# Loads and gathers pinned to the program's order, weight writes in 32 parts

## The chip, the cores and the metric

One core of one Trainium2 chip runs one program. The metric is the device time of an execution in microseconds (us). Of the kernel before there are three runs; the profile is a fourth execution with the hardware profiler on. The program is written with a scheduler that places each engine's instructions itself, out of an estimate of when their inputs are ready; the order in which the program traces them is only a priority, unless an edge is added.

## What is computed

A transformer block over 512 tokens of width 2048 in float32: adaptive norm, a mixer (forgetting attention and a gated linear recurrence), and a feed-forward part with 16384 experts, of which each token uses 16 in each of 8 heads. The change lies in the last:

```python
def _peer(h, w_q, k1, k2, u, vt):
    q = (h @ w_q).reshape(B, S, PEER_HEADS, 2, PEER_HALF)
    s1, s2 = (einsum of q's halves with k1 and with k2)
    ...                     # top 16 of each, top 16 of the 256 sums
    e = expert numbers      # 8 heads x 16 for each token
    w = softmax of the sums
    def expert_block(hx, ex, wx):
        ug = jnp.take(u, ex, axis=0)
        act = jax.nn.gelu(jnp.einsum('thkd,td->thk', ug, hx)) * wx
        vg = jnp.take(vt, ex, axis=0)
        return jnp.einsum('thk,thkd->td', act, vg)
```

## The kernel before

Matrix products run as three passes over float32 values that are split into a high part (cast by ScalarE, L93) and a low part (subtracted by VectorE, L94). `stream` (L96) loads 512 KB into `raw` (four slots) and splits it into `shi` and `slo` (three slots each).

For three of the four groups of 128 tokens the kernel doesn't gather rows of u. It multiplies all of u with the tokens: 128 blocks of 128 experts, `ublock` (L682). A block is two streamed halves of `peer_u`, 24 matmuls each (L689), into a PSUM bank of the two named pj; then gelu on ScalarE (L693), and two writes of the result `ge` to tables in memory through SyncE's queue, to tab2 (L695) and to tab1 (L697). `ublocks(upto)` runs blocks until that number; its calls are spread over the program, so that blocks are traced between other work. This is the block stage, about 1085 to 2385 us.

Beside the blocks run:

- The side work for the fourth group of tokens: 256 gathers of 128 rows (1 MB each) by GpSimd (L743, L766), each used by one VectorE instruction (L755 or L757). `pump`, called after each half of a block, releases 0.9 of them on average, and one scatter.
- `halves_of` (L896): the routing weights of 64 tokens over all experts, `ws`, made by one-hot matmuls (L912) and copied by ScalarE (L913), written to the tables by four writes of 1 MB in rows of 256 bytes (L917) and reduced by VectorE (L918). It is called for three groups, two halves each, with one buffer for `ws`.
- `make_list` (L832): for each row of 128 experts of a block, the numbers of the blocks in use, sorted by 16 rounds of `V.max` and `V.match_replace` (`rounds`, L818), and 16 or 20 scatters of list entries by GpSimd (`one`, L882); `done` (L886) reads the list back through SyncE.
- A top-k for the third group's scores, read back from memory in eight loads (L931).

After the last block the rows of v are gathered chunk by chunk and multiplied (L988). The scheduler decides what stands where in SyncE's list: peer_u loads, writes of ge, writes of ws and the small loads all go through it.

Of the kernel before, what the change touches and what calls it, by code (L numbers as in the profile page):

```python
# [27 lines left out]
LISTS = ((48, 16, 4), (66, 20, 5))  # L28
NONE = 24
B0 = 3  # L30
BH = 18
BL = 20
GRATE = 0.9
GLAG = 2
NAR = 5
# [23 lines left out]
def program(ctx: ExitStack, tc: tile.TileContext, a):  # L59
    nc = tc.nc  # L60
    V, A, PE, G = nc.vector, nc.scalar, nc.tensor, nc.gpsimd
# [31 lines left out]
        A.copy(hi, src)  # L93
        V.tensor_tensor(out=lo, in0=src, in1=hi, op=OP.subtract)  # L94

    def stream(src, n=1024):  # L96
        r = raw.tile([128, 1024], F32, name="raw")
        nc.sync.dma_start(r[:, :n], src)
        hi = hl.tile([128, 1024], F32R, name="shi")
        lo = hl.tile([128, 1024], F32R, name="slo")  # L100
        hilo(hi[:, :n], lo[:, :n], r[:, :n])
        return hi, lo
# [32 lines left out]
    for half in range(2):  # L135
        r = raw.tile([128, 1024], F32, name="raw")[:1]
# [34 lines left out]
    for q in range(4):  # L171
        p = pbank()
# [7 lines left out]
    with tc.tile_pool(name="pro", bufs=1, reuse_waits="tile") as pro:  # L180
# [7 lines left out]
        for t in range(NT):  # L188
# [7 lines left out]
            r = rstd(pro, ss, 1, 1.0 / D)  # L196
            dg = pro.tile([128, 128], F32, name="dg", bufs=2)
            V.tensor_scalar(dg, ident, r, None, op0=OP.mult)
            for k4 in range(4):
                p = pbank()  # L200
# [62 lines left out]
    p = pbank()  # L263
# [9 lines left out]
    p = bank()  # L273
# [245 lines left out]
    for q in range(4):  # L519
# [8 lines left out]
        for k2 in range(KC // 2):  # L528
            w = stream(a["w_out"][q, k2])
# [8 lines left out]
        for t in range(NT):  # L538
# [10 lines left out]
            if q == 3:  # L549
                s4 = const.tile([128, 1], F32, name="s4", bufs=4)  # L550
                V.tensor_reduce(s4, ssq[:, t], axis=AX.X, op=OP.add)
                w = const.tile([128, 128], F32, name="dg", bufs=4)
# [6 lines left out]
    with tc.tile_pool(name="wk2", bufs=12, reuse_waits="tile") as wk2:  # L559
        for q in range(4):  # L560
            pr = bank()
            for k4 in range(4):
                k = q * 4 + k4
                p = bank()
# [80 lines left out]
    for h in range(H):  # L645
# [6 lines left out]
        for half in range(2):  # L652
            p = pbank()
            for hv in range(2):
                wh, wl = stream(a["w_q"][h * 2 + half, hv])
                for k8 in range(8):
                    k = hv * 8 + k8
# [6 lines left out]
            p = bank()  # L664
            c0 = half * 128
# [16 lines left out]
    def ublock(b):  # L682
        p = pbank()
        for half in range(2):
            uh, ul = stream(a["peer_u"][b, half])
            for k8 in range(8):
                k = half * 8 + k8
                for i, (l, r) in enumerate(three(uh, ul, dh[k], dl[k])):
                    PE.matmul(p[:, :NDT], l[:, k8 * 128:k8 * 128 + 128], r, start=(k == 0 and i == 0),  # L689
                              stop=(k == KC - 1 and i == 2))  # L690
            pump()
        ge = gq.tile([128, NDT], F32, name="ge")
        A.activation(ge, p[:, :NDT], AF.Gelu_apprx_tanh)  # L693
        rows = slice(128 + b * 128, 256 + b * 128)
        nc.sync.dma_start(tab2[rows].rearrange("p (t x) -> p t x", t=2)[:, :, 0:128],  # L695
                          ge[:, 128:384].rearrange("p (t x) -> p t x", t=2))
        nc.sync.dma_start(tab1[rows, 0:128], ge[:, 0:128])  # L697
# [5 lines left out]
    blk = [0]  # L703
    todo = []
# [5 lines left out]
    def ublocks(upto):  # L710
        while blk[0] < upto:
            ublock(blk[0])
            blk[0] += 1
# [9 lines left out]
    ei = late.tile([128, H * 16], I32, name="ei")  # L723
# [16 lines left out]
    tabs = (tab2, tab1)  # L740

    def gather(out, src, idx):
        G.indirect_dma_start(out=out, out_offset=None, in_=src,  # L743
                             in_offset=bass.IndirectOffsetOnAxis(ap=idx, axis=0))

    NSIDE = 2 * H * 16 + GLAG

    def side_work():
        held = []
        n = H * 16  # L750

        def use():
            v, j, r = held.pop(0)
            if v:
                V.scalar_tensor_tensor(out=y0, in0=r, scalar=dots[:, j:j + 1], in1=y0, op0=OP.mult, op1=OP.add)  # L755
                return
            V.scalar_tensor_tensor(out=r, in0=r, scalar=1.0, in1=hrow, op0=OP.mult, op1=OP.mult,  # L757
                                   accum_out=dots[:, j:j + 1])
            if j == n - 1:
                A.activation(dots, dots, AF.Gelu_apprx_tanh)  # L760
                V.tensor_tensor(out=dots, in0=dots, in1=ew, op=OP.mult)

        for v in range(2):
            for j in range(n):
                r = gb.tile([128, D], F32, name="gr")
                gather(r, a["v_rows" if v else "u_rows"], ei[:, j:j + 1])  # L766
                held.append((v, j, r))
                if len(held) > GLAG:
                    use()
                yield  # L770
        while held:
            use()
            yield
# [16 lines left out]
    def scatter_some(n):  # L790
        for _ in range(n):
            if scatters:
                scatters.pop(0)()

    todo.append(lambda: side.send(GRATE))
    todo.append(lambda: scatter_some(1))
    for t in (1, 2):
# [20 lines left out]
    def rounds(L, vals, n):  # L818
        for k in range(n):
            sl = slice(k * 8, k * 8 + 8)  # L820
            V.max(L[:, sl], vals[k % 2])
            V.match_replace(vals[1 - k % 2], L[:, sl], vals[k % 2], 0.0)
        return vals[n % 2]

    def rows_of(L, n, nm):
# [6 lines left out]
    def make_list(lt, Fs, n):  # L832
        c0, r, _ = LISTS[n]
        own = []
        cnt = lt.tile([128, 2], F32, name="lcnt")
        vals = [lt.tile([128, 128], F32, name=f"lv{i}") for i in range(2)]
        L = lt.tile([128, 128], F32, name="lf")
# [5 lines left out]
        else:  # L843
# [4 lines left out]
            for i, f in enumerate(fs):  # L848
                rest = rounds(L, [f, vals[0]], NONE // 8)
                ig, iv = rows_of(L, NONE, f"own{i}")  # L850
# [7 lines left out]
        ig, iv = rows_of(L, 128, n)  # L858
# [3 lines left out]
        p = bank()  # L862
# [13 lines left out]
        idx = lp1.tile([128, 32], I32, name=f"lidx{n}")[:, :r]  # L876
# [3 lines left out]
        sv = lp1.tile([128, r], I32, name=f"sv{n}")  # L880

        def one(i):  # L882
            G.indirect_dma_start(out=views[i], out_offset=bass.IndirectOffsetOnAxis(ap=idx[:, i:i + 1], axis=0),
                                 in_=ig[:, c0 + i:c0 + i + 1], in_offset=None, bounds_check=128 * r - 1, oob_is_err=False)

        def done():  # L886
            nc.sync.dma_start(sg, lists[n].rearrange("(p c) o -> p (c o)", p=128))
# [5 lines left out]
    TH = 64  # L893
    sets = {}

    def halves_of(dz, t, o, tab, c0, lo, step):  # L896
        Fs = []
        for hf in range(2):
            h0 = hf * TH
            ws = dz.tile([128, NB, TH], F32, name="ws")  # L900
            for t4 in range(TH // 4):
                ublocks(lo + hf * step + t4 * (step - 3) // (TH // 4))
                p = bank()
                o1 = dz.tile([128, 4, 128], F32, name="o1", bufs=2)
                t0 = h0 + t4 * 4
                V.tensor_tensor(out=o1, in0=iota[:, None, :].to_broadcast([128, 4, 128]),
                                in1=o[:, 0, t0:t0 + 4, None].to_broadcast([128, 4, 128]), op=OP.is_equal)
                for j in range(4):
                    tt = t0 + j
                    o2 = dz.tile([128, 128], F32, name="o2", bufs=6)  # L910
                    V.tensor_scalar(o2, iota, o[:, 1, tt:tt + 1], o[:, 2, tt:tt + 1], op0=OP.is_equal, op1=OP.mult)
                    PE.matmul(p[:, j * 128:j * 128 + 128], o2, o1[:, j], start=True, stop=True)  # L912
                A.copy(ws[:, :, t4 * 4:t4 * 4 + 4].rearrange("p i t -> p t i"), p.rearrange("p (t i) -> p t i", t=4))  # L913
            F = dz.tile([128, NB], F32, name="F", bufs=4)
            for i in range(4):
                sl = slice(i * 32, i * 32 + 32)
                nc.sync.dma_start(tab[128 + i * 4096:4224 + i * 4096, c0 + h0:c0 + h0 + TH].rearrange("(i p) t -> p i t", p=128), ws[:, sl])  # L917
                V.tensor_reduce(F[:, sl], ws[:, sl], axis=AX.X, op=OP.max)  # L918
            Fs.append(F)
        V.tensor_tensor(out=Fs[0], in0=Fs[0], in1=Fs[1], op=OP.max)  # L920
        return Fs[0]
# [191 lines left out]
    r = inv(1)  # L1113
# [75 lines left out]
```

## Time and profile before

| | |
|---|---|
| median of three runs | 3143.48 us (3142.44 to 3146.86) |
| the profiled execution, its span | 3144.75 us, 3142.9 us |
| TensorE busy | 2872.5 us (91%) |
| VectorE busy | 2487.0 us (79%) |
| ScalarE, GpSimd busy | 1220.9 us (39%), 944.1 us (30%) |
| loads of peer_u | 256 of 512 KB |
| writes of ge | 128 of 128 KB, 128 of 64 KB |
| writes of ws | 24 of 1 MB |
| gathers of the side work, scatters | 256, 36 |

In the rows PE is TensorE, PEld its weight loads, DVE VectorE, ACT ScalarE, POOL GpSimd, SP SyncE; a q behind the name is that engine's sequencer, where DMAs are issued and waits are held. L12 is line 12 of the kernel. A row names output<-input by the program's names. "[1.37 <-DMA ...]" is the engine's idle time ahead of the instruction and what ended it. PEclk is the granted clock of TensorE, 1.00 for 2.4 GHz and 0.50 for 1.2 GHz.

### The profile page before, as it was taken

How to read it: one execution, taken by the hardware profiler on the slowest of the kernel's cores; microseconds unless marked ns; L12 is line 12 of the kernel's file. 1: busy time of each engine (PE TensorE's matmuls, PEld its weight loads, DVE VectorE, ACT ScalarE, POOL GpSimd, SP SyncE). 2: the span in 40 equal slices, each digit the busy share in tenths (PEclk: the TensorE clock that was granted, in tenths of full speed). 3: DMA queues.
4: the chain of work that ended last, by engine and by line, in shares of the span. 5: the costliest groups of instructions: out<-in, count | busy, mean ns of one | idle time of the engine just before them, and what ended most of it. 6: DMA issues, size and time to landing. Idle time of an engine off the chain costs nothing.

```text
span 3142.9 us, 39160 instructions
## 1 busy us (share of the span) xinstructions
PE 2872.5 (91%) x14093; PEld 2501.5 (80%) x14093; DVE 2487.0 (79%) x4100; ACT 1220.9 (39%) x1653; POOL 944.1 (30%) x673
## 2 busy tenths in 40 slices
PE   7899999989999999988878999889998899988887
PEld 5677777778788899988868999879996688766665
DVE  6877777763368899999989998968888866677787
ACT  5322223662232333433322343413223455556665
POOL 0000000000020033222242322264447645567774
PEclk9999899999999999999988999989999999999998
DMA  9867777333322389999989999989999977779896
GB/s 343 291 222 235 239 236 238 106 107 128 114 90 94 117 297 379 340 306 295 294 270 357 351 347 352 314 319 404 404 403 386 386 278 272 260 270 344 320 327 228
DMA packets 329503, 869.31 MB, mean 277 GB/s; under 512 B 125682, under 2 KB 181362, under 8 KB 274388
## 3 DMA queue, kind: packets, MB, share of 16 engines
q0 software_dynamic: 72512, 477.03, 40.4%
q1 hardware_dynamic: 256352, 389.52, 36.8%
q8 instruction: 112, 1.84, 0.2%
q14 instruction: 91, 0.75, 0.1%
q10 hardware_dynamic: 436, 0.18, 0.0%
HBM read 805.38 MB, written 61.25 MB: 276 GB/s over the span
## 4 chain that ended last, share of the span: by engine, by line
PE 53%; DVE 17%; DMA 15%; issue 8%; ACT 3%; POOL 2%; SPq 1%; DVEq 0%; POOLq 0%; ACTq 0%
PE pj L689 25%; DMA araw<-w_ada 8%; PE ps L988 7%; PE pj L659 6%; DVE slo L94 5%; PE ps L525 4%; DVE gr L757 3%; PE pj L301 2%; PE ps L219 2%; DMA raw<-tab,ig 2%; DVE araw L147 2%; PE ps L912 2%; PE pj L988 1%; PE pj L525 1%; DMA tab<-ws 1%
## 5 line engine op out<-in xcount | busy, mean ns | idle before, releaser
L689 PE MATMUL pj<-dh,slo 128*128 128x384 f32 x2048 | 698.3, 343 | 59.4 <-DVE slo L94 57.9
L689 PE MATMUL pj<-dh,shi 128*128 128x384 f32 x2048 | 699.1, 341 | 29.0 <-ACT shi L93 26.4
L689 PE MATMUL pj<-dl,shi 128*128 128x384 f32 x2048 | 694.8, 339 | 1.3 <-issue 1.3
L93 ACT CAST shi<-raw 128x1024 fp32r<-128x1024 f32 (+1 forms) x402 | 418.3, 1048 | 634.1 <-PE pj L689 219.0
L94 DVE TENSOR_TENSOR slo<-raw,shi 128x1024 fp32r<-128x1024 f32 (+1 forms) x402 | 485.1, 1214 | 214.3 <-ACT shi L93 200.1
L689 PEld LDWEIGHTS pj<-dh,slo 128*128 128x128 f32 x2048 | 392.1, 192 | 70.6 <-DVE slo L94 68.7
L94 DVE TENSOR_TENSOR slo<-gr,shi 128x1024 fp32r<-128x1024 f32 x342 | 407.2, 1220 | 39.6 <-ACT shi L93 38.1
L689 PEld LDWEIGHTS pj<-dh,shi 128*128 128x128 f32 x2048 | 393.0, 192 | 30.9 <-ACT shi L93 27.9
L93 ACT CAST shi<-gr 128x1024 fp32r<-128x1024 f32 x342 | 345.0, 1046 | 157.0 <-PE ps L988 99.2
L743 POOL DMA_INDIRECT gr<-u_rows,ei x128 | 196.0, 1531 | 690.5 <-DVE gr L757 319.6
L689 PEld LDWEIGHTS pj<-dl,shi 128*128 128x128 f32 x2048 | 392.3, 192 | 2.1 <-issue 2.0
L988 PE MATMUL ps<-shi,gh 128*128 128x512 f32 x740 | 277.7, 418 | 64.3 <-ACT gh L93 36.7
L147 DVE SCALAR_TENSOR_TENSOR araw<-araw,sil 128x1024 f32<-128x1024 f32 x192 | 233.7, 1222 | 104.8 <-DMA araw<-w_ada 101.5
L755 DVE SCALAR_TENSOR_TENSOR y<-gr,dots,y 128x2048 f32<-128x2048 f32 x128 | 300.3, 2346 | 13.9 <-DMA gr<-v_rows,ei 12.6
L988 PE MATMUL ps<-slo,gh 128*128 128x512 f32 x740 | 298.0, 411 | 14.6 <-DVE slo L94 13.8
L743 POOL DMA_INDIRECT gr<-v_rows,ei x128 | 211.7, 1654 | 311.4 <-DVE y L755 204.6
L757 DVE SCALAR_TENSOR_TENSOR gr<-gr,hrow 128x2048 f32<-128x2048 f32 x128 | 291.5, 2279 | 11.3 <-DMA gr<-u_rows,ei 8.8
L988 PE MATMUL ps<-shi,gl 128*128 128x512 f32 x740 | 273.8, 401 | 2.1 <-DVE gl L94 2.1
L678 POOL CAST dh<-hh 128x384 fp32r<-128x384 f32 x16 | 10.3, 645 | 857.8 <-DVE hh L572 857.8
L693 ACT ACTIVATE ge<-pj 128x384 f32<-128x384 f32 x128 | 63.0, 492 | 459.0 <-PE pj L689 371.1
L988 PEld LDWEIGHTS ps<-shi,gh 128*128 128x128 f32 x740 | 145.5, 198 | 112.2 <-ACT gh L93 45.7
L301 PE MATMUL pj<-hh,shi 128*128 128x512 f32 x528 | 215.6, 408 | 3.9 <-ACT w L477 3.5
(353 smaller groups left out, 4966.7 us busy)
## 6 DMA issues: line engine op xcount, KB each, us to landing
raw<-peer_u SPq DMA_DIRECT2D x256, 512.0 KB
araw<-w_ada SPq DMA_DIRECT2D x192, 512.0 KB
raw<-w_in SPq DMA_DIRECT2D x66, 512.0 KB
tab<-ws SPq DMA_DIRECT2D x24, 1024.0 KB
raw<-w_out SPq DMA_DIRECT2D x32, 512.0 KB
raw<-w_q SPq DMA_DIRECT2D x32, 512.0 KB
tab<-ge SPq DMA_DIRECT2D x128, 128.0 KB
tab<-ge SPq DMA_DIRECT2D x128, 64.0 KB
```

The source lines that it names most:

```text
L93: A.copy(hi, src)
L94: V.tensor_tensor(out=lo, in0=src, in1=hi, op=OP.subtract)
L147: V.scalar_tensor_tensor(out=r, in0=r, scalar=1.0, in1=sil[:, half * 1024:half * 1024 + 1024], op0=OP.mult, op1=OP.mult, accum_out=acc[:, ...
L301: PE.matmul(p, l[:, k8 * 128:k8 * 128 + 128], r, start=(k == 0 and i == 0), stop=(k == KC - 1 and i == 2))
L525: PE.matmul(po[t], l[:, ts], r[:, sl], start=(k == 0 and i == 0), stop=(k == KC - 1 and i == 2))
L659: PE.matmul(p, l[:, k8 * 128:k8 * 128 + 128], r, start=(k == 0 and i == 0), stop=(k == KC - 1 and i == 2))
L689: PE.matmul(p[:, :NDT], l[:, k8 * 128:k8 * 128 + 128], r, start=(k == 0 and i == 0), stop=(k == KC - 1 and i == 2))
L693: A.activation(ge, p[:, :NDT], AF.Gelu_apprx_tanh)
L743: G.indirect_dma_start(out=out, out_offset=None, in_=src, in_offset=bass.IndirectOffsetOnAxis(ap=idx, axis=0))
L755: V.scalar_tensor_tensor(out=y0, in0=r, scalar=dots[:, j:j + 1], in1=y0, op0=OP.mult, op1=OP.add)
L757: V.scalar_tensor_tensor(out=r, in0=r, scalar=1.0, in1=hrow, op0=OP.mult, op1=OP.mult, accum_out=dots[:, j:j + 1])
L988: PE.matmul(banks[t][half * 2 + q2], l[:, ts], x[:, sl], start=first and i == 0, stop=end and i == 2)
```

## The change

`tc.keep_in_program_order(ins)` adds an edge from the instruction that was traced last on the same engine to `ins`: `ins` is issued after it. It adds no wait for that one's end.

- Each load of peer_u is pinned in this way on SyncE, each gather of the side work and each scatter on GpSimd, and each round's `V.max` on VectorE.
- The four writes of a half's `ws` become 32, queued in `slices`; `pump` issues four of them after each half of a block, each pinned. Five blocks are left behind the one-hot matmuls of a half, the last of them called after the reduction.
- After each fourth of the 16 sorting rounds, except the last, one block is traced.
- The blocks' positions move: 17 blocks to a half in place of 18 and 20. Their number stays 128.

```diff
--- before.py
+++ after.py
@@ -28,8 +28,9 @@
 LISTS = ((48, 16, 4), (66, 20, 5))
 NONE = 24
 B0 = 3
-BH = 18
-BL = 20
+BH = 17
+BL = 17
+ROUNDS = 4
 GRATE = 0.9
 GLAG = 2
 NAR = 5
@@ -93,9 +94,11 @@
         A.copy(hi, src)
         V.tensor_tensor(out=lo, in0=src, in1=hi, op=OP.subtract)
 
-    def stream(src, n=1024):
+    def stream(src, n=1024, pin=False):
         r = raw.tile([128, 1024], F32, name="raw")
-        nc.sync.dma_start(r[:, :n], src)
+        load = nc.sync.dma_start(r[:, :n], src)
+        if pin:
+            tc.keep_in_program_order(load)
         hi = hl.tile([128, 1024], F32R, name="shi")
         lo = hl.tile([128, 1024], F32R, name="slo")
         hilo(hi[:, :n], lo[:, :n], r[:, :n])
@@ -682,7 +685,7 @@
     def ublock(b):
         p = pbank()
         for half in range(2):
-            uh, ul = stream(a["peer_u"][b, half])
+            uh, ul = stream(a["peer_u"][b, half], pin=True)
             for k8 in range(8):
                 k = half * 8 + k8
                 for i, (l, r) in enumerate(three(uh, ul, dh[k], dl[k])):
@@ -740,8 +743,8 @@
     tabs = (tab2, tab1)
 
     def gather(out, src, idx):
-        G.indirect_dma_start(out=out, out_offset=None, in_=src,
-                             in_offset=bass.IndirectOffsetOnAxis(ap=idx, axis=0))
+        return G.indirect_dma_start(out=out, out_offset=None, in_=src,
+                                    in_offset=bass.IndirectOffsetOnAxis(ap=idx, axis=0))
 
     NSIDE = 2 * H * 16 + GLAG
 
@@ -763,7 +766,7 @@
         for v in range(2):
             for j in range(n):
                 r = gb.tile([128, D], F32, name="gr")
-                gather(r, a["v_rows" if v else "u_rows"], ei[:, j:j + 1])
+                tc.keep_in_program_order(gather(r, a["v_rows" if v else "u_rows"], ei[:, j:j + 1]))
                 held.append((v, j, r))
                 if len(held) > GLAG:
                     use()
@@ -792,6 +795,14 @@
             if scatters:
                 scatters.pop(0)()
 
+    slices = []
+
+    def slices_some(n):
+        for _ in range(n):
+            if slices:
+                slices.pop(0)()
+
+    todo.append(lambda: slices_some(4))
     todo.append(lambda: side.send(GRATE))
     todo.append(lambda: scatter_some(1))
     for t in (1, 2):
@@ -818,8 +829,10 @@
     def rounds(L, vals, n):
         for k in range(n):
             sl = slice(k * 8, k * 8 + 8)
-            V.max(L[:, sl], vals[k % 2])
+            tc.keep_in_program_order(V.max(L[:, sl], vals[k % 2]))
             V.match_replace(vals[1 - k % 2], L[:, sl], vals[k % 2], 0.0)
+            if k % ROUNDS == ROUNDS - 1 and k < n - 1:
+                ublocks(blk[0] + 1)
         return vals[n % 2]
 
     def rows_of(L, n, nm):
@@ -880,8 +893,8 @@
         sv = lp1.tile([128, r], I32, name=f"sv{n}")
 
         def one(i):
-            G.indirect_dma_start(out=views[i], out_offset=bass.IndirectOffsetOnAxis(ap=idx[:, i:i + 1], axis=0),
-                                 in_=ig[:, c0 + i:c0 + i + 1], in_offset=None, bounds_check=128 * r - 1, oob_is_err=False)
+            tc.keep_in_program_order(G.indirect_dma_start(out=views[i], out_offset=bass.IndirectOffsetOnAxis(ap=idx[:, i:i + 1], axis=0),
+                                 in_=ig[:, c0 + i:c0 + i + 1], in_offset=None, bounds_check=128 * r - 1, oob_is_err=False))
 
         def done():
             nc.sync.dma_start(sg, lists[n].rearrange("(p c) o -> p (c o)", p=128))
@@ -899,7 +912,7 @@
             h0 = hf * TH
             ws = dz.tile([128, NB, TH], F32, name="ws")
             for t4 in range(TH // 4):
-                ublocks(lo + hf * step + t4 * (step - 3) // (TH // 4))
+                ublocks(lo + hf * step + t4 * (step - 5) // (TH // 4))
                 p = bank()
                 o1 = dz.tile([128, 4, 128], F32, name="o1", bufs=2)
                 t0 = h0 + t4 * 4
@@ -912,10 +925,15 @@
                     PE.matmul(p[:, j * 128:j * 128 + 128], o2, o1[:, j], start=True, stop=True)
                 A.copy(ws[:, :, t4 * 4:t4 * 4 + 4].rearrange("p i t -> p t i"), p.rearrange("p (t i) -> p t i", t=4))
             F = dz.tile([128, NB], F32, name="F", bufs=4)
+            def write(i, ws=ws, c=c0 + h0):
+                tc.keep_in_program_order(nc.sync.dma_start(
+                    tab[128 + i * 512:640 + i * 512, c:c + TH].rearrange("(i p) t -> p i t", p=128), ws[:, i * 4:i * 4 + 4]))
+
+            slices.extend([lambda i=i, w=write: w(i) for i in range(32)])
             for i in range(4):
                 sl = slice(i * 32, i * 32 + 32)
-                nc.sync.dma_start(tab[128 + i * 4096:4224 + i * 4096, c0 + h0:c0 + h0 + TH].rearrange("(i p) t -> p i t", p=128), ws[:, sl])
                 V.tensor_reduce(F[:, sl], ws[:, sl], axis=AX.X, op=OP.max)
+            ublocks(lo + hf * step + step)
             Fs.append(F)
         V.tensor_tensor(out=Fs[0], in0=Fs[0], in1=Fs[1], op=OP.max)
         return Fs[0]
```

## Rows read from the trace of the kernel before

**Rows 1.** Busy time by stretch: engines (instructions), clock, DMA share, GB/s; block stage.
```profile
core 0: us, PE busy (x) PEld busy (x) DVE busy (x) ACT busy (x) POOL busy (x), PEclk, DMA share, GB/s
1085.00:2385.00 1300.00, 1194.47 (x6900) 1176.72 (x6899) 1179.78 (x1633) 420.42 (x501) 445.94 (x284) 0.96 0.94 337
```

**Rows 2.** Waits of PE, 1085 to 2385: waiter, releaser, us, times, longest.
```profile
PE pj L689 <- DVE slo L94: 57.9, 27, 9.2
PE pj L689 <- ACT shi L93: 26.4, 8, 9.3
```

**Rows 3.** Pieces of the chain of waits: start, us, what.
```profile
1282.84 1.14 DVE slo L94
...
1284.03 4.43 PE pj L689 x24
...
1464.97 8.32 PE pj L689 x48
```

**Rows 4.** The write L695 in the whole run: ns min/median/max, first and last start.
```profile
L695 SPq DMA_DIRECT2D tab<-ge x128: 524/525/9519, 1088.3 to 2383.4; - x128
```

**Rows 5.** SyncE's DMA queue in order of time: start, us, line, transfer, count.
```profile
1041.39 5.80 SPq L98 DMA_DIRECT2D raw<-peer_u  x2
...
1079.57 2.97 SPq L98 DMA_DIRECT2D raw<-peer_u  x2
...
1088.28 0.62 SPq L695 DMA_DIRECT2D tab<-ge  x1
1088.95 0.59 SPq L697 DMA_DIRECT2D tab<-ge  x1
1089.63 3.69 SPq L98 DMA_DIRECT2D raw<-peer_u  x2
1095.19 0.54 SPq L695 DMA_DIRECT2D tab<-ge  x1
```

**Rows 6.** Waits of SyncE's queue, 1085 to 2385.
```profile
SPq L695 <- ACT ge L693: 347.8, 99, 8.4
```

**Rows 7.** ScalarE in order of time: the gelu of one block.
```profile
1094.68 0.48 ACT L693 ACTIVATE ge<-pj 128x384 f32<-128x384 f32 x1
```

**Rows 8.** SyncE's DMA queue: loads of 512 KB in three stages.
```profile
418.58 3.12 SPq L146 DMA_DIRECT2D araw<-w_ada  x2
1016.34 5.80 SPq L98 DMA_DIRECT2D raw<-w_q  x2
1158.16 0.33 SPq L98 DMA_DIRECT2D raw<-peer_u  x1
```

**Rows 9.** Busy time by stretch: two earlier stages, and two us after a load.
```profile
400.00:430.00 30.00, 29.06 (x133) 23.36 (x133) 19.46 (x36) 8.78 (x14) 0.00 (x0) 1.00 0.73 238
960.00:1080.00 120.00, 120.00 (x579) 100.02 (x578) 99.31 (x408) 31.08 (x42) 0.00 (x0) 1.00 0.30 99
1018.00:1019.00 1.00, 1.00 (x6) 0.82 (x5) 1.00 (x6) 0.40 (x1) 0.00 (x0) 1.00 0.92 365
1019.00:1020.00 1.00, 1.00 (x7) 0.85 (x6) 1.00 (x7) 0.64 (x1) 0.00 (x0) 1.00 0.01 4
```

**Rows 10.** ScalarE and VectorE in order of time: users of two of these loads.
```profile
423.85 1.23 DVE L147 SCALAR_TENSOR_TENSOR araw<-araw,sil 128x1024 f32<-128x1024 f32 x1 [1.37 <-DMA araw<-w_ada]
1166.25 1.05 ACT L93 CAST shi<-raw 128x1024 fp32r<-128x1024 f32 x1 [2.46 <-DMA raw<-peer_u]
```

**Rows 11.** TensorE in order of time: matmuls behind a gap (gap and releaser in brackets).
```profile
1352.62 0.69 PE L689 MATMUL pj<-dh,slo 128*128 128x384 f32 x1 [4.95 <-DVE slo L94]
1353.11 0.52 PE L689 MATMUL pj<-dh,shi 128*128 128x384 f32 x1
1353.43 0.52 PE L689 MATMUL pj<-dl,shi 128*128 128x384 f32 x1
...
1356.91 0.34 PE L689 MATMUL pj<-dh,shi 128*128 128x384 f32 x1
```

**Rows 12.** SyncE's DMA queue: one set of weight writes and the load behind.
```profile
1338.30 17.48 SPq L917 DMA_DIRECT2D tab<-ws  x4
1355.88 9.68 SPq L98 DMA_DIRECT2D raw<-peer_u  x1
```

**Rows 13.** Busy time by stretch: list 0, its scatters and the next top-k.
```profile
1585.00:1685.00 100.00, 74.10 (x390) 71.94 (x389) 88.38 (x258) 19.54 (x24) 41.82 (x31) 0.86 0.88 303
```

## The prediction

> **What bounds the kernel now.** I first cut the span into stretches and read engine times. The change lies in the block stage, 1085 to 2385 us: in its 1300 us TensorE is busy for 1194.5 and VectorE for 1179.8, and the DMA engines are 94% busy [rows 1]. So TensorE sets the pace and at most 1300 - 1194.5 = 105.5 us of it are idle. The waits of TensorE name these: 57.9 us for the low parts of VectorE (L94), 26.4 us for the casts of ScalarE (L93) [rows 2]. A block of 48 matmuls takes 8.32 us when nothing is in its way [rows 3]; from the first block's write to the last's there are 127 steps in 2383.4 - 1088.3 = 1295.1 us [rows 4], 10.2 us each; the rest is the one-hot matmuls of L912 and the idle time.
>
> What makes this pace possible is how far the loads run ahead. In the DMA queue of SyncE eight loads of peer_u (four blocks) are issued before the write of block 0's result (L695, L697), and the two after that write are block 4's [rows 5]. SyncE takes its list in order: 99 times it stands at L695 until the gelu of ScalarE has written ge, 347.8 us in all [rows 6]. Today that costs nothing, as the loads behind the write are for a block that TensorE reaches three blocks later.
>
> **The change, part by part.**
>
> Pinned loads. keep_in_program_order places a load behind the instruction that the program traced last on SyncE. For the first half of block b+1 that is L697 of block b, the second write of its ge. So this load can be issued only after the last matmul of block b, its gelu and both writes; the lead of four blocks becomes none. raw has four slots and hl three, but they no longer help. The second half follows the first at once (no instruction between, or four slices), and its load and casts lie beside the 4 us of the first half's matmuls. The cost of one step, from a block's last matmul on:
> - gelu: 0.48 us from 1094.68 [rows 7], 0.1 before it as an estimate and 0.03 to the write at 1095.19; the two writes put the load's issue 1089.63 - 1088.28 = 1.35 us behind L695's [rows 5]. Together 1.96.
> - issue to landing. No load here stands alone, so bounds: in the quiet w_q stage (DMA share 0.30) a load issued at 1016.34 has its packets over by 1019, 2.7 us [rows 8, 9]. In the block stage a load issued at 1158.16 is cast at 1166.25, as soon as it has landed: 8.1 us [rows 8, 10]. Between them, at a share of 0.73, a load of the same size issued at 418.58 is used at 423.85: 5.3 us [rows 8 to 10]. After the change the bytes of the stage are the same (0.94 x 1300 = 1222 us of DMA time) over some 2390 us, a share of 0.51; half way between 0.30 and 0.73 is 4.0, and since gathers come in bursts I take 4.3.
> - cast 1.05 us [rows 10], low part 1.14, and 0.05 to the matmul [rows 3]; two matmuls can run on the high part meanwhile, 0.35 less: 1.89.
> - the block itself, 8.32 [rows 3], and its clock: after the 4.95 us gap at 1347.67 the matmuls come 0.32 us apart until 1356.6, that is 13 of them at half clock (1.2 GHz) instead of 0.173 [rows 11]: 13 x 0.147 = 1.9 more. The new gap is 8.1 us, so I charge it in every block.
> Sum: 1.96 + 4.3 + 1.89 + 8.32 + 1.9 = 18.37 us a step, 127 x 18.37 = 2333 against 1295: **+1038 us**. With the ends of the landing (2.7 with 1.2 of slow clock, and 8.1) a step takes 16.1 or 22.2 us: +745 or +1520.
>
> The Trainium skill (DMA: Bandwidth & Descriptors, section Anatomy of one DMA — SWDGE (gpsimd) path) says that a DMA engine doesn't wait on semaphores and that the issuing sequencer does so before dispatch; the 99 waits of SyncE at L695 agree [rows 6]. The same section has a fixed 2.0 us and 436 GB/s; an estimate from it for 512 KB is 3.2 us, with which the sum would be +898.
>
> What this swallows: the gap of 8.1 us a step takes in the one-hot matmuls of L912 and VectorE's side work, so the 105 us of today's idle time and the one-hots aren't added again. VectorE needs 1179.8 / 128 = 9.2 us a block [rows 1] and is no longer near the bound.
>
> Routing weights in 32 parts. Before, four writes of 1 MB keep SyncE for 17.48 us, and the load behind them needs 9.68 us to issue [rows 12]; six such sets explain much of the waits above. After, 192 parts of 128 KB, by bytes 17.48 / 32 = 0.55 us each, four behind each half's load. They put the second load 2.2 us later; it is then ready about 0.4 + 2.2 + 1.2 (transfer) = 3.8 us after the first, inside the 6 us that the first half's matmuls take at the mixed clock. Cover gone, 2 us in 24 blocks: bounds 0 to 48, taken 20. The stall removed lay in idle time that the new gap swallows, so no gain.
>
> GpSimd in program order. The 36 scatters and 256 gathers keep their number. What can be won is TensorE's idle time where list 0's scatters ran ahead of the gathers: 1585 to 1685 has 26 idle us [rows 13]. What can be lost: a gather behind a scatter whose index VectorE still computes. Both lie under the new gap: 0, bounds -26 to +26.
>
> Sort in four parts and moved blocks (17 for 18 and 20). Three blocks come between the sort's parts, but between list 0 and the eighth head of the next top-k no block is left to run: the load of block 74 is behind that head's load. The nearest row is again the 26 us of [rows 13]; I take +25, bounds 0 to 40.
>
> Total 1038 + 20 + 25 = +1083. The profiled execution took 3144.75 us (span 3142.9), the median 3143.48; 3144.75 + 1083 = 4228, 1.3 less on the median's scale: about **4230 us**. The stages before 1085 and after 2385 are left as they are.
>
> **The rivals.**
> - Faster: the pin orders loads and parts among themselves but not behind the write of ge, and the loads keep their lead. Then 32 small parts and the spread sort take away up to two thirds of the 105 us: about 3075 us. The point that decides is whether a load of block b+1 stands ahead of L697 of block b in SyncE's list. Against it: L697 is on SyncE and is traced right before that load.
> - More contention: VectorE is now idle half the time, so gathers run ahead and are always in flight; each landing costs the 8.1 us of today's full queues. 22.2 us a step: 4710 us. For it: [rows 10]. Against: only one pair of loads is then in flight, not four blocks' worth.
> - The clock never recovers: 48 x 0.32 = 15.4 us a block in place of 10.2, 23.5 a step: 4880 us. Against: at 1356.91 it is back while the stage goes on [rows 11].
> - The change does nothing, because the scheduler had this order anyway: 3143. Against: the eight loads ahead of the first write [rows 5].
>
> The Trainium skill (TensorE: Matmul & The Clock Gate, section HAM oscillation — how this bites in real kernels) says that a loop whose bursts of matmuls wait for a DMA each time starts every burst throttled, which is the 1.9 us in all 127 steps; rows 11 show it for one gap, no run here for a loop of them. If the clock held, 127 x 1.9 = 241 us would fall away: 3990.
>
> **How the numbers follow.** Forecast 0.75, contention 0.09, low clock 0.05, loads keep their lead 0.09, nothing 0.02. Within 0.2% counts as no change, about what a measurement of this kernel can tell. Faster 0.09, same 0.02, slower 0.89. The range holds the forecast with its bounds and the contention case: 3950 to 4710; outside are the faster case, no change and the low clock, 0.16, and little more at the lower edge.
>
> **What would show it.** SyncE's list: one pair of peer_u loads between each L697 and the next L695, the first right behind L697. ScalarE's casts: every second one waits for a load, some 120 times. TensorE: 127 gaps of 6 to 9 us, then a dozen matmuls 0.32 us apart. DMA share in the stage near 0.5, VectorE under 0.6. I am wrong if loads stand ahead of the write, or if the step isn't 16 to 22 us: then the landing or the clock is what to look at.

## The result, and the profile after

The kernel after takes 4450.58 us (median of six runs, 4438.30 to 4461.63) against 3142.96 us: 1.417 times, interval 1.413 to 1.421. The prediction was 4230, 3950 to 4710. The profiled execution took 4438.3 us with a span of 4436.5 us, 1293.6 more than before.

First the page: the engines' totals, the granted clock and the DMA share in 40 slices.

```profile
PE 3185.1 (72%) x14093; PEld 2721.0 (61%) x14093; DVE 2509.5 (57%) x4100; ACT 1235.4 (28%) x1652; POOL 969.7 (22%) x673
...
PEclk9998999999666677787786778777777779999999
DMA  9677724331688873322449832243533227998886
```

TensorE's busy time grew by 313 us with the same work, because the clock fell in the middle of the span (mean 0.846, before 0.958). The stretches show that only the block stage changed: it now lasts until 3690 (columns as in [rows 1]).

```profile
1085.00:1665.00 580.00, 299.39 (x1342) 273.60 (x1341) 465.80 (x585) 93.47 (x105) 213.08 (x130) 0.70 0.75 283
1665.00:2300.00 635.00, 397.49 (x1853) 368.63 (x1852) 184.56 (x309) 119.19 (x136) 25.20 (x19) 0.80 0.31 97
2300.00:3690.00 1390.00, 820.00 (x3735) 762.09 (x3735) 531.99 (x704) 223.29 (x259) 221.00 (x130) 0.78 0.43 149
1085.00:3690.00 2605.00, 1516.88 (x6929) 1404.32 (x6927) 1182.35 (x1597) 435.95 (x500) 459.29 (x277) 0.77 0.48 166
3690.00:4436.00 746.00, 655.77 (x2676) 510.29 (x2676) 573.65 (x757) 402.10 (x547) 489.60 (x358) 0.96 0.86 323
```

The fourth row answers to [rows 1]: 2605 us for what took 1300, VectorE at the same 1180 us of work and now mostly idle, TensorE idle for 1088 us, DMA share 0.48. The three rows above it split the stage: early on the gathers run (DMA 0.75), then they don't (0.31). The write of ge, line L698 now, answers to [rows 4]:

```profile
L698 SPq DMA_DIRECT2D tab<-ge x128: 521/525/615, 1092.4 to 3687.2; - x128
```

127 steps in 2594.8 us, 1299.7 more than before: the whole difference. (The stage starts 4 us later, and what follows it is 10 us shorter.) One step is 20.43 us in the mean and 18.39 in the median; before, 10.20 and 9.04. Mean steps below are made in this way from the line's first and last start, medians from its 128 starts. Blocks are counted from 0, and the step at block b ends with its write.

What ends the waits, 1085 to 3690, of SyncE's queue, TensorE and ScalarE (waiter, releaser, us, times, longest), answering to [rows 2, 6]:

```profile
SPq L698 <- ACT ge L696: 1956.4, 122, 32.6
...
PE pj L692 <- ACT shi L94: 890.7, 128, 18.3
PE pj L692 <- DVE slo L95: 91.4, 119, 7.4
...
ACT ge L696 <- PE pj L692: 1113.1, 123, 19.4
ACT shi L94 <- DMA raw<-peer_u: 884.8, 225, 16.6
```

Read together they are a ring: SyncE waits for the gelu, ScalarE's cast for the load, TensorE for the cast, the gelu for TensorE. Before, SyncE's wait was 347.8 us [rows 6] and cost nothing. SyncE's queue in order of time shows what closes the ring, answering to [rows 5]:

```profile
2075.00 0.53 SPq L698 DMA_DIRECT2D tab<-ge  x1
2075.58 0.60 SPq L700 DMA_DIRECT2D tab<-ge  x1
2076.27 0.87 SPq L99 DMA_DIRECT2D raw<-peer_u  x2
2092.19 0.53 SPq L698 DMA_DIRECT2D tab<-ge  x1
```

One pair of loads, right behind the second write of ge, and then nothing until the next gelu: the lead of [rows 5], where eight loads stand ahead of the first write, is gone. So it is in 125 of the 127 steps. The other two, at blocks 74 and 77, show the reverse:

```profile
2681.66 1.82 SPq L99 DMA_DIRECT2D raw<-peer_u  x4
2697.93 0.53 SPq L698 DMA_DIRECT2D tab<-ge  x1
...
2705.91 0.52 SPq L698 DMA_DIRECT2D tab<-ge  x1
```

Four loads are issued together, those of block 73 and those of block 74, and the writes of the two blocks are 7.97 us apart. Block 74 is the first one traced after the last read of the third group's scores (L949), so its load is pinned behind that read and not behind block 73's write; the read was issued at 2626.35. Within one run, the step without the wait for the write thus stands beside the step with it. What block 77's load is pinned behind isn't shown. The step that begins at 2075.00, on ScalarE and on TensorE, in order of time (gap and its releaser in brackets), answers to [rows 7, 10, 11]:

```profile
2074.49 0.49 ACT L696 ACTIVATE ge<-pj 128x384 f32<-128x384 f32 x1 [9.69 <-PE pj L692]
2079.83 1.04 ACT L94 CAST shi<-raw 128x1024 fp32r<-128x1024 f32 x1 [4.85 <-DMA raw<-peer_u]
...
2074.11 0.34 PE L692 MATMUL pj<-dh,slo 128*128 128x384 f32 x1
2080.92 0.69 PE L692 MATMUL pj<-dh,shi 128*128 128x384 f32 x1 [6.47 <-ACT shi L94]
2081.41 0.52 PE L692 MATMUL pj<-dl,shi 128*128 128x384 f32 x1
...
2084.59 0.46 PE L692 MATMUL pj<-dh,shi 128*128 128x384 f32 x1
2084.88 0.34 PE L692 MATMUL pj<-dl,shi 128*128 128x384 f32 x1
```

From the load's issue at 2076.27 to its cast at 2079.83 are 3.56 us, and behind the gap some ten matmuls run at the half clock before they come at the spacing of the full one again (2084.88).

### The profile page after: what moved, and what is told of

Its sections match the earlier page's. It is cut to its first block, busy times and chain, and to the rows that moved or that the text cites. A ratio compares the mean times of both kernels' runs of the same rounds, so it can differ in the third digit from the quotient of the medians.

```text
span 4436.5 us, 39261 instructions
## 1 busy us (share of the span) xinstructions
PE 3185.1 (72%) x14093; PEld 2721.0 (61%) x14093; DVE 2509.5 (57%) x4100; ACT 1235.4 (28%) x1652; POOL 969.7 (22%) x673
## 5 line engine op out<-in xcount | busy, mean ns | idle before, releaser
L692 PE MATMUL pj<-dh,shi 128*128 128x384 f32 x2048 | 813.4, 397 | 899.9 <-ACT shi L94 892.5
L692 PEld LDWEIGHTS pj<-dh,shi 128*128 128x128 f32 x2048 | 469.4, 229 | 938.9 <-ACT shi L94 929.3
L692 PE MATMUL pj<-dh,slo 128*128 128x384 f32 x2048 | 801.3, 391 | 92.6 <-DVE slo L95 92.5
L692 PE MATMUL pj<-dl,shi 128*128 128x384 f32 x2048 | 784.9, 383 | 0.0
L692 PEld LDWEIGHTS pj<-dh,slo 128*128 128x128 f32 x2048 | 456.4, 223 | 152.2 <-DVE slo L95 151.8
L692 PEld LDWEIGHTS pj<-dl,shi 128*128 128x128 f32 x2048 | 467.5, 228 | 0.0
L746 POOL DMA_INDIRECT gr<-u_rows,ei x128 | 212.3, 1659 | 512.7 <-PE pj L692 208.7
L1006 PE MATMUL ps<-shi,gh 128*128 128x512 f32 x740 | 257.1, 410 | 68.7 <-ACT gh L94 39.3
L896 POOL DMA_INDIRECT list<-ig,lidx x36 | 47.0, 1305 | 1131.3 <-DVE iv L842 1121.0
L304 PE MATMUL pj<-hlo,shi 128*128 128x512 f32 x528 | 214.4, 406 | 0.0
```

The lines of the kernel that those rows point to most:

```text
L304: PE.matmul(p, l[:, k8 * 128:k8 * 128 + 128], r, start=(k == 0 and i == 0), stop=(k == KC - 1 and i == 2))
L746: return G.indirect_dma_start(out=out, out_offset=None, in_=src, in_offset=bass.IndirectOffsetOnAxis(ap=idx, axis=0))
L896: tc.keep_in_program_order(G.indirect_dma_start(out=views[i], out_offset=bass.IndirectOffsetOnAxis(ap=idx[:, i:i + 1], axis=0), in_=ig[:, ...
L1006: PE.matmul(banks[t][half * 2 + q2], l[:, ts], x[:, sl], start=first and i == 0, stop=end and i == 2)
```

## The experiments

"After" is the kernel after. Each time stands beside that of the kernel before on the same chip (its median there, in brackets).

**a_nopin: is the pin of the loads the cause?** After, without that one edge.

```diff
-            uh, ul = stream(a["peer_u"][b, half], pin=True)
+            uh, ul = stream(a["peer_u"][b, half])
```

> The changed kernel with the pin of the peer_u loads alone taken away; GpSimd's order, the sort in four parts, the 32 parts of the weight writes and the moved blocks stay. Theory (the load of block b+1 stands behind the write of block b's result): the loads get their lead of four blocks back, the step from one write to the next falls from 20.4 us to about 10, and the time to between 3060 and 3160 us. Rival (the small weight writes or GpSimd's order cost the 1300 us): it stays above 4000 us.

Measured: 3173.08 us (3140.09), 1.010, interval 1.007 to 1.014; 1277 us of the 1308 are gone, and a step is 10.52 us (median 9.66). Its waits, 1085 to 2450:

```profile
SPq L698 <- ACT ge L696: 378.0, 96, 8.7
...
PE pj L692 <- ACT shi L94: 56.7, 16, 19.0
PE pj L692 <- DVE slo L95: 47.4, 41, 11.6
```

SyncE waits about as long as before [rows 6], and TensorE little, as in [rows 2]. The pin is necessary for the loss. The rest of the change isn't free either: the time is 13 us over the expected range.

**b_pinonly: is it sufficient?** Before, with the pin and nothing else.

```diff
-        nc.sync.dma_start(r[:, :n], src)
+        load = nc.sync.dma_start(r[:, :n], src)
+        if pin:
+            tc.keep_in_program_order(load)
...
-            uh, ul = stream(a["peer_u"][b, half])
+            uh, ul = stream(a["peer_u"][b, half], pin=True)
```

> The kernel before with nothing but the pin of the peer_u loads. Theory: this alone makes the slowdown; the four large weight writes stand in front of a load again and add up to 6 x 17 us, so 4350 to 4600 us. Rival (the pin only hurts together with the weight parts that stand between the loads): below 3500 us.

Measured: 4405.16 us (3140.09), one execution. The write's line (L697 here):

```profile
L697 SPq DMA_DIRECT2D tab<-ge x128: 524/525/9909, 1091.2 to 3675.6; - x128
```

20.35 us a step, median 17.72. The time is in the expected range: the pin alone makes the loss. Neither the 32 parts nor the order of GpSimd is needed for it.

**c_geact: is it the wait of the write, or the pin as such?** After, with both writes of ge on ScalarE's queue; the pinned loads then have no write of ge ahead of them.

```diff
-        nc.sync.dma_start(tab2[rows].rearrange("p (t x) -> p t x", t=2)[:, :, 0:128],
+        nc.scalar.dma_start(tab2[rows].rearrange("p (t x) -> p t x", t=2)[:, :, 0:128],
...
-        nc.sync.dma_start(tab1[rows, 0:128], ge[:, 0:128])
+        nc.scalar.dma_start(tab1[rows, 0:128], ge[:, 0:128])
```

> The changed kernel with the two writes of each block's result issued from ScalarE's queue in place of SyncE's; all pins stay, so a load is now behind the load or the weight part traced before it and behind no write of a result. Theory: no load waits for a gelu any more, lead and pace come back: 3060 to 3200 us, the upper end if issuing two writes a block costs ScalarE 1.2 us beside its casts. Rival (pinned loads are slow by themselves, whatever stands ahead of them): above 4000 us.

Measured: 3323.51 us (3140.09), 1.058, interval 1.055 to 1.061. The median step is 8.80, as good as before's, so the wait of the write was the mechanism. But the time is 124 us above the range. Three long steps, called holes below, hold more than that: blocks 3 (86.0 us), 74 (75.9) and 77 (68.9). SyncE's wait at the first of them, and its queue there and at the second (columns as above):

```profile
SPq L822 <- DVE padi L825: 72.4, 1, 72.4
```

```profile
1153.22 0.33 SPq L822 DMA_DIRECT2D tab<-pad  x1
...
1155.88 41.58 SPq L99 DMA_DIRECT2D raw<-peer_u  x10
...
1942.66 13.77 SPq L949 DMA_DIRECT2D s<-sspill  x3
1973.95 0.33 SPq L900 DMA_DIRECT2D sg<-list  x1
```

At these two the pinned load stands behind what else is on SyncE's queue: the padding of the tables and lists (L822 to L827), which waits for VectorE, then the reads of the third group's scores and of the list (L949, L900), which wait too. What the scheduler would have moved ahead stands in line. The third hole is of another kind. The load of block 77 is issued at 2010.31, and its cast begins only at 2084.72, because ScalarE stands at a copy of the third group's top-k ahead of it:

```profile
2079.29 0.48 ACT L735 COPY oT<-ps 128x384 f32<-128x384 f32 x1 [39.99 <-PE ps L734]
...
2084.72 1.99 ACT L94 CAST shi<-raw 128x1024 fp32r<-128x1024 f32 x2
```

That copy waits for transposes on TensorE (L734), which wait 26.8 and 20.2 us for VectorE. In after it is over at 2662.62, five blocks earlier.

**d_lag1, d_lag2: how far ahead must the load be?** After, with the writes of block b traced one or two blocks later (for two, `gq` gets three slots and `gwp` two), all on SyncE and all pins kept.

```diff
+        behind.append((rows, ge))
+        if len(behind) > LAG:
+            write_ge()
+
+    def write_ge():
+        rows, ge = behind.pop(0)
         nc.sync.dma_start(tab2[rows].rearrange("p (t x) -> p t x", t=2)[:, :, 0:128],
```

> The changed kernel with the writes of a block's result traced one block later, so that the loads of block b+1 stand behind the writes of block b-1. Theory: the load gets a lead of one block's 8.3 us of matmuls, and from the write to the low part the median step needs 1.3 + 4.05 + 1.08 + 1.2 = 7.6 us; the median step falls to about 10 us, but the steps whose landing takes 8 to 15 us still wait: 3150 to 3350 us. Rival (the cost is the order as such and not the lost lead): above 4000 us.

> As the run with the writes of a block's result traced one block later, now two blocks later (three slots for the result, and two in place of three for the weights of the last stage). Theory: loads get a lead of two blocks; the median step goes from 9.8 to 8.4 to 9.0 us and the mean from 12.75 to below 12; the holes behind the padding and the score loads stay, since they aren't the result's writes: 3330 to 3420 us. Rival (the lead no longer matters after one block): 3460 us or more.

The write's line, in d_lag1 and in d_lag2:

```profile
L707 SPq DMA_DIRECT2D tab<-ge x128: 524/525/4907, 1095.3 to 2714.9; - x128
```

```profile
L707 SPq DMA_DIRECT2D tab<-ge x128: 524/525/5602, 1094.6 to 2609.9; - x128
```

Measured:

| blocks between a write and its place | time (before) | median step | mean step |
|---|---|---|---|
| 0: after | 4450.58 (3142.96) | 18.39 | 20.43 |
| 1: d_lag1 | 3471.22 (3140.09) | 9.84 | 12.75 |
| 2: d_lag2, one execution | 3348.43 (3152.72) | 9.21 | 11.93 |
| loads free: a_nopin | 3173.08 (3140.09) | 9.66 | 10.52 |

One block of distance gives the median step back almost in full, as it must if the load waits for that write. With one block the time is 121 us over the expected range: the holes at blocks 3 (81.2 us) and 77 (67.0) stand where c_geact has them, and 29 steps take 15 to 25 us (in c_geact 9). With two blocks the time and the mean fell in the expected range; the median, 9.21, is over its 8.4 to 9.0.

**e_nogather: what do the gathers add to the step?** After, without the 256 gathers of the side work; its VectorE instructions run on one zeroed tile, so the fourth group's experts are left out of the output.

```diff
+        r = gb.tile([128, D], F32, name="gr")
+        V.memset(r, 0.0)
...
-                r = gb.tile([128, D], F32, name="gr")
-                tc.keep_in_program_order(gather(r, a["v_rows" if v else "u_rows"], ei[:, j:j + 1]))
```

> The changed kernel without the 256 gathers of the side work: its 256 VectorE instructions run on one zeroed tile, so the fourth group of tokens lacks its experts. Theory (the steps of 24 to 34 us, which raise the mean from the median 18.4 to 20.4 us, are loads that share the DMA engines with gathers, and low parts that queue behind their users): all steps come near 17.5 to 18.2 us, the landing's mean near 3.6 us, and the last write comes some 300 us earlier: 4060 to 4180 us, of which the missing gathers behind the last block explain at most 60. Rival (VectorE's fixed order makes the long steps, whatever the DMA engines do): the mean step stays above 19.5 us and the time above 4300 us.

Measured: 4293.05 us (3140.22), one execution, over the range and just under the rival's bounds (its mean step is 19.37 us). From the issue of a block's first load to its cast are now 3.95 us in the mean (after 5.13). The worst is 7.25 us at block 74, where four loads are issued together as in after; apart from blocks 74 and 77 it is 4.73 (in after 15.29, or 15.17 where the cast waits for nothing but its load). The stage, and SyncE's wait at block 3:

```profile
1085.00:3640.00 2555.00, 1585.93 (x7269) 1462.77 (x7268) 1295.30 (x1726) 478.94 (x557) 85.79 (x81) 0.79 0.28 86
```

```profile
SPq L822 <- DVE padi L825: 98.2, 1, 98.2
```

The DMA share fell from 0.48 to 0.28 and the landings with it, but the step at block 3 grew to 119.4 us: the padding (L822) waits 98 us for VectorE, and the loads stand behind it. Without block 3 a step is (2460.4 - 119.4) / 126 = 18.58 us, in after (2594.8 - 53.4) / 126 = 20.17: the gathers, with the waits of VectorE for them, are worth 1.6 us a step, some 200 us. The median step, 18.25, is nearly that of after: a quiet step doesn't meet a gather.

**f_warm: what does the clock cost?** After, with 30 matmuls behind each block that nobody reads, to keep TensorE at work in the gap.

```diff
+        if b < NB - 1:
+            w = bank()
+            for i in range(WARM):
+                tc.keep_in_program_order(PE.matmul(w[:, :NDT], dh[0][:, :128], dh[0], start=i == 0, stop=i == WARM - 1))
```

> The changed kernel with 30 further matmuls of 128x384 behind each block, on tiles that are there anyway, whose result nobody reads: 30 x 0.173 = 5.2 us of the gap of some 8 us are filled. Theory (each block pays about 1.9 us because its first matmuls run at 1.2 GHz after the gap): the granted clock of the block stage goes from 0.77 to above 0.95, the median step from 18.4 to 16.3 to 16.9 us, the time to 4180 to 4280 us. Rival (the slow clock isn't on the path, or the added matmuls delay the next block): 4400 us or more.

Measured: 4484.83 us (3140.22), one execution, in the rival's range. The stage:

```profile
1085.00:3700.00 2615.00, 2006.19 (x10532) 1923.42 (x10530) 1156.26 (x1535) 427.83 (x483) 432.90 (x266) 0.88 0.47 163
```

The clock of the stage rose from 0.77 to 0.88 only. In the quiet steps, from the first half's low part to the gelu took 8.3 to 8.6 us, against 9.4 to 9.8 in after (tenth to fortieth percentile of each): about 1.1 to 1.2 us, below the 1.9 of the sum. The median step fell from 18.39 to 17.89; the time didn't fall, since landings grew (6.02 us in the mean, 5.13 in after), the steps with landings over 4.5 us still took 10.2 us for this stretch (after 10.3), and holes opened at blocks 74 (79.8 us) and 77 (44.0). So the clock term is real, but this run does not give its size over the whole stage.

**g_geact_few: do the holes of c_geact go if fewer loads are pinned?** c_geact, with a load pinned only while parts of the weight writes are still queued.

```diff
-            uh, ul = stream(a["peer_u"][b, half], pin=True)
+            uh, ul = stream(a["peer_u"][b, half], pin=bool(slices))
```

> The changed kernel with the writes of a block's result on ScalarE's queue, and loads pinned only while parts of the weights wait to be written. The run with those writes moved showed three holes of 69 to 86 us in which pinned loads stood behind other entries of SyncE's list (the zero padding, the reading back of scores and list). Theory: these holes go, some 200 us, and what is left is the pace of the other steps, 8.8 us in the median: 3090 to 3150 us. Rival (the holes come from the work itself, not from the list's order): above 3250 us.

Measured: 3295.46 us (3140.22), 1.049, interval 1.047 to 1.052: a miss, in the rival's range. The holes at 3, 74 and 77 are gone (6.9, 8.8 and 8.0 us), but the steps at blocks 14 and 88, 38.9 and 35.1 us in c_geact, now take 120.1 and 127.9. Its wait row, 1085 to 2600:

```profile
SPq L929 <- ACT ws L926: 184.6, 2, 110.5
```

Here the loads stand behind the first weight parts, which wait for the copies of `ws`. Inside the second hole ScalarE's wait for the third group's transposes stands again, 40.0 us as in c_geact. So the work that is waited for stayed, and another instruction of the queue passed the wait on to the loads. Where no load is pinned (a_nopin) the same two steps take 6.7 and 7.2 us; how much of the holes is the order and how much the work isn't separated.

**h_nopin_nogps, i_gps, j_fourwrites: what are the other parts worth?** a_nopin without GpSimd's pins; before with GpSimd's pins alone; and a_nopin with the four writes of 1 MB in place of the 32 parts (so GpSimd's order, the sort in four and the moved blocks).

The edit of h (on the gathers; that on the scatters is alike, and i makes both the other way round):

```diff
-                tc.keep_in_program_order(gather(r, a["v_rows" if v else "u_rows"], ei[:, j:j + 1]))
+                gather(r, a["v_rows" if v else "u_rows"], ei[:, j:j + 1])
```

The edit of j, beside that of a_nopin:

```diff
-            slices.extend([lambda i=i, w=write: w(i) for i in range(32)])
...
+                nc.sync.dma_start(tab[128 + i * 4096:4224 + i * 4096, c0 + h0:c0 + h0 + TH].rearrange("(i p) t -> p i t", p=128), ws[:, sl])
```

> The changed kernel without the pins of the loads and without those of GpSimd's gathers and scatters; left are the sort in four parts, the 32 parts of the weight writes with their pins, and the moved blocks. Theory (GpSimd's order neither wins nor loses much): within 1% of the run without the load pins, 3140 to 3205 us. Rival (GpSimd's order is what makes that run 1% slower than the kernel before): 3130 us or less.

> The kernel before with nothing but GpSimd's gathers and scatters pinned to the program's order. Theory (taking these pins out of the run without load pins cost 28 us, 3173 to 3201, as scatters and gathers no longer wait at the wrong place): 3105 to 3140 us, faster than before by up to 1%. Rival (that gain hung on the sort in four parts or on the weight parts): 3140 to 3170 us.

> The changed kernel without the pins of the loads and with the four writes of 1 MB in place of the 32 parts: GpSimd's order, the sort in four parts and the moved blocks are left. Theory (the 32 pinned parts stand in SyncE's list where they wait, and this is what makes the run without load pins 1% slower than the kernel before): 3100 to 3145 us. Rival (the moved blocks and the sort in parts are the 1%): 3165 us or more.

| kernel | time (before) | ratio, interval |
|---|---|---|
| a_nopin | 3173.08 (3140.09) | 1.010, 1.007 to 1.014 |
| h: a without GpSimd's pins | 3201.24 (3140.22) | 1.020, 1.018 to 1.023 |
| i: before with GpSimd's pins | 3124.14 (3152.72) | 0.991, 0.989 to 0.994 |
| j: a with four writes | 3117.98 (3152.72) | 0.990, 0.988 to 0.992 |

All three fell in their expected ranges. The ratios are compared, since not all of these runs were on one chip. GpSimd's order gains 0.9% over before (i) and 1.0% within a_nopin (a against h). The 32 parts lose 2% (a against j). The sort in four and the moved blocks change nothing that can be measured (j against i). So j_fourwrites is 1.0% faster than the kernel before, and i_gps, a change of a few lines, is as fast. What an edit changes by itself, and what the scheduler changes in answer to it, these runs don't tell apart. The block stage of j, answering to [rows 1], and its writes:

```profile
1085.00:2385.00 1300.00, 1200.53 (x6921) 1181.87 (x6920) 1151.65 (x1610) 427.38 (x504) 419.26 (x278) 0.96 0.93 329
```

```profile
L698 SPq DMA_DIRECT2D tab<-ge x128: 524/525/8424, 1083.7 to 2358.8; - x128
```

TensorE is idle for 99.5 of 1300 us, before 105.5 [rows 1], and the 127 steps take 1275.1 us in place of 1295.1. How the parts cost their 2% in a_nopin wasn't tried further.

## Why the prediction was right, point by point

**The mechanism held.** In 125 of 127 steps the load stands behind L700, one pair between two writes; TensorE has its gaps with slow matmuls behind them; the DMA share is 0.48 for "near 0.5". So it was foretold, and a, b, c and d leave the wait of the write as the cause. Two signs came out differently. Loads do stand ahead of the write at blocks 74 and 77. And ScalarE waits for a load at 225 casts, not at every second one: 117 first halves for 704 us, 108 second halves for 181. The rivals fall: the loads kept no lead but for those two; contention cost 8 us and more only in part of the steps; the clock recovers inside a block (2084.88). The price of the first was also off: with the lead kept and all other edits in, a_nopin takes 3173 us, not 3075; TensorE's idle time in the 127 steps didn't fall from 104 us to a third but rose to 135.

**The sum, term by term.** From the 127 steps of the trace of after, in us:

| term | predicted | median | mean | mean minus predicted, x 127 |
|---|---|---|---|---|
| L698's issue to the load's issue | 1.35 | 1.27 | 1.13 | -28 |
| load's issue to cast | 4.3 | 4.05 | 5.13 | +105 |
| cast's start to low part's start | 1.05 | 1.08 | 1.76 | +90 |
| low part | 1.14 | 1.23 | 1.22 | +10 |
| its end to the gelu (block and clock) | 10.02 | 10.07 | 10.60 | +74 |
| gelu to L698 | 0.51 | 0.52 | 0.59 | +10 |
| step | 18.37 | 18.39 | 20.43 | +262 |

(10.02 is 8.32 + 1.9 + 0.05 + 0.1 - 0.35.) The median step is the predicted one to 0.02 us. That close it is in part luck: no median is off by more than 0.25 us, but the medians of the terms add up to 18.22, and 4.3 was a choice inside bounds of 2.7 and 8.1. What the sum lacked is the tail. The 45 us that it added for parts and sort are to be taken off the 262: 217 us too little, which is 1299.7 less 1083.

**Two terms were mis-sized.** The landing: 4.3 was a mean from a DMA share of 0.51 spread evenly. The trace has 0.75 until 1665 and 0.31 after [the stretches above], and 27 steps over 24 us, all but one in blocks 2 to 22, 57 to 65 and 95 to 98, where gathers run ahead; there landings take up to 15.2 us; all 23 of 8 us and more have a gather in flight. My contention rival was thus right for a fifth of the steps: it should have been a term with a share, not a case for all. e_nogather bears this out with 1.6 us a step. The low part: I took VectorE as idle half the time and so free; over all it is (1182 of 2605 us), but its side work comes in bursts, and a low part then waits up to 9 us for it (0.7 us in the mean; 0.5 remain without gathers, 1.62 against 1.08).

**The clock term** of 1.9 us came from 13 slow matmuls [rows 11]; here the quiet step has some ten, and f_warm gave back some 1.1 to 1.2. The median of the block term, 10.07 against 10.02, hides that this one was a little large and the rest a little small. The Trainium skill (TensorE: Matmul & The Clock Gate, section HAM oscillation — how this bites in real kernels) has every burst behind a wait for a DMA start throttled; the step shown above agrees, with 0.32 us between matmuls until 2084.59. The prediction's time for a held clock, 3990, was not reached by f_warm, which did not hold it.

**The landing beside its estimate.** It was 3.3 us at the least and 3.5 in the lowest tenth of the steps. The estimate of 3.2 us by the Trainium skill (DMA: Bandwidth & Descriptors, section Anatomy of one DMA — SWDGE (gpsimd) path) is close to these quiet ones and 1.9 below the mean. The section gives its figures for DMAs that GpSimd issues, and these loads are SyncE's, so the agreement is no test of it. The measurement decides, and the sum with 4.3 was nearer than that with 3.2.

**The top-k's +25 had the wrong place and the wrong sign.** The load of block 74 is behind the eighth head's read, as foretold, but that read had been issued 56 us before (2626.35 and 2682.64). Being pinned there freed the load from the write: the step takes 7.97 us, 10.4 less than the median, and the one at block 77 the same. The hole came at block 3, where the load is pinned behind the padding (SyncE's queue in after, and its wait):

```profile
1140.27 0.60 SPq L700 DMA_DIRECT2D tab<-ge  x1
1156.71 0.32 SPq L822 DMA_DIRECT2D tab<-pad  x1
...
1159.39 1.06 SPq L99 DMA_DIRECT2D raw<-peer_u  x2
```

```profile
SPq L822 <- DVE padi L825: 15.8, 1, 15.8
```

That step is 53.4 us, 35 more than the median: 18.4 from the late load, and most of the rest from its cast and low part, which came late too (15.29 and 6.0 us in place of 4.05 and 1.08). I had listed the write of ge as what is traced last on SyncE, and had not gone through the other instructions that come last on it. In c_geact and d_lag2 the reads of the top-k do hold the loads up (75.9 and 78.9 us at block 74), so the place was possible; in after the last of them is issued 56 us before that load.

**GpSimd's order at 0 and the 32 parts at +20** weren't measured each by itself under the pin. b_pinonly, without them and without the sort in four and the moved blocks, takes 45 us less than after, in one execution; how that divides is open. Without the pin, GpSimd's order alone gains 28.6 us (i_gps), a little over the bound of 26, and the parts cost 2%.

**Open:** how f_warm's loss divides between the low clock and its new holes, and why the holes move between blocks 3, 14, 74, 77 and 88 from kernel to kernel. Every edit makes the scheduler place the work anew, but no run shows which placement makes which hole.

## What to carry to other kernels

An order edge costs no wait of its own, but on a queue taken in order it hands the load the wait of what was traced last before it: list all instructions that can stand there, the writes of results first, and look at what each waits for. If loads must be pinned, keep the write of the result that they help to make on another queue, or trace it a block or two later. Here even that left the kernel 6% (c_geact, d_lag2) or 10% (d_lag1) slower than before, and loads left free were best. GpSimd's own order, where no such write stands, could be pinned with a gain of 0.9%. And when a step is put on the critical path, sum it for the quiet and for the crowded stretches apart, with a share for each, since a mean DMA share or a mean load of VectorE tells nothing of its bursts.

## What the runs showed of the hardware

In after, the first load of 512 KB of a pair reached its user 3.3 to 4.5 us after its issue in seven steps of ten, and took 8 to 15 us in 23 steps, each with a gather in flight; in e_nogather it took at most 4.73 us, but for the two steps with four loads issued together (5.7 and 7.3). In f_warm, thirty matmuls of filler in each gap raised the granted clock of the stage from 0.77 to 0.88 and not to the 0.96 of [rows 1]. A write of ge takes ScalarE's sequencer as long to issue in c_geact as SyncE's in after, 521 ns against 525 in the median; the median step of c_geact, 8.80 us, shows no loss from it.
